# Where the matmul operands of a decoder layer start in SBUF: gaps between pools

## The chip, the cores and the metric

One NeuronCore of a Trainium2 chip runs the whole kernel as one program. The metric is device time in microseconds, the median of several runs. Before the change it is 1307.95 us (3 runs, 1306.92 to 1308.1). The profiled execution took 1307.29 us by the clock of the runs; the span from its first to its last instruction is 1305.5 us, so 1.8 us lie around the span.

## The reference, cut to what matters

One decoder layer in float32 on 1024 tokens plus 16 meta tokens (L = 1040), width 1024:

```
a    = rmsnorm(h, ln_mix_pre);  proj = a @ w_in            # 1024 x 3584
mix  = concat(diff_attention(...), hgrn2(...)) @ w_out      # 1024 x 1024: the output projection
h    = h + rmsnorm(mix, ln_mix_post)
a    = rmsnorm(h, ln_ffn_pre)
u    = causal_depthwise_conv3(a @ w_up) + conv_b            # 1024 x 5632: the up stage
gate, up = split(u)
y    = (gelu(gate) * up) @ w_down                           # 2816 x 1024: the down stage
out  = h + rmsnorm(y, ln_ffn_post), meta rows dropped
```

## The kernel before, in words

**Split products.** Every large matrix product runs in float32r, with both operands split into a high part and a low part. A product of a stationary operand S and a moving operand M is three matmuls into one PSUM bank: S high with M high, S high with M low, S low with M high (or with the roles exchanged). They always stand next to each other in the program, and each matmul loads its own 128 columns of stationary operand (512 bytes in each partition) ahead of itself: 'PEld' in the profile is that load, 'PE' the matmul.

**The stages on TensorE**, in the order of the program:

- The input projection (L234, L236, L238): the weights are stationary, the normalized activations `ahi` and `alo` move, 272 or 384 columns at a time. A row of `ahi` is 1040 floats, 4160 bytes, so that from one of its 8 rows k to the next the start moves by 64 bytes modulo 512. Attention and HGRN heads are interleaved with it.
- The output projection (`out_part`, L1012, L1014, L1016): blocks of the mixed heads (`mp`, loaded back from DRAM into X1, X2 or the pool `mixload`; `m7` in the pool `early`) are stationary, `w_out` moves, 512 columns at a time. Its first half (`out_first`) is interleaved with the last HGRN head; the second half alternates with a residual and norm chain (`post`, `trans`).
- The up stage (`unit`, L1378 to L1380): one level of Strassen's scheme (Winograd's form). For each of 21 tiles `ft` and both column groups p there are seven products j = 0 to 6 of 12 matmuls. Weights `uh`, `ul` (pools `weights` and `sums`, in turns) are stationary; the activation tile `t{p}_{j}` moves. A tile holds 4 rows of high parts and then 4 rows of low parts. For p = 0 a row has 258 columns, for p = 1 it has 256. The tiles lie in several pools: `early` (e0, e1), the `mix` tiles X0, X1, X2, `tsplit` and `tsplit2`. The p = 1 tile in X0, `t1_6`, is stored with rows of 258 columns, of which 256 are used.
- `plain_unit` (L1359 to L1361) computes tile ft = 0 without the scheme while the sums for the seven tiles are still being made.
- The down stage (L1536 to L1538): again seven products, 77 steps of 12 matmuls; the gated activations `gh`, `gl` (pool `down`) are stationary, the weights `wh`, `wl` (pool `weights`) move, 512 columns at a time. 924 matmuls in all.

**What sets the addresses.** A tile pool takes SBUF when it is opened, from the left end or the right end, next to the pool that was opened before on that side and is still open. Inside a pool the tiles stand one behind the other in the order in which they are first asked for. So one tile's size decides where everything behind it starts. Nearly every tile is a multiple of 512 bytes in each partition or a known remainder above it, so the distance between two operands modulo 512 is fixed for a whole stage.

**The word distance below** is the start of the moving operand minus the start of the stationary operand, in bytes within a partition, modulo 512. It is worked out from the addresses in the built program, which the profile does not show. As one row of weights is 512 bytes and one weight tile 2048, it is the same for the stationary operand that is used and the one that is loaded next, as long as the tile stays the same.

Of the kernel before, what the change touches and what calls it, by code (L numbers as in the profile page):

```python
# [9 lines left out]
F32 = mybir.dt.float32  # L10
F32R = mybir.dt.float32r
# [6 lines left out]
P = 128  # L18
META = 16
SEQ = 1024  # L20
L = META + SEQ
D = 1024
KD = D // P
# [8 lines left out]
WN = [258, 256]  # L32
# [53 lines left out]
def layer_kernel(ctx: ExitStack, tc: tile.TileContext, x, meta, table, lbl, gpre, gpost, win,  # L86
# [25 lines left out]
    def const(shape, name, dt=F32):  # L112
        return cp.tile(shape, dt, tag=name, name=name)
# [12 lines left out]
    nlam = const([P, 1], "nlam")  # L126
    cwt = const([P, 2 * NF, 3], "cwt")
    cbt = const([P, 2 * NF], "cbt")
    m0 = const([P, 152], "m0", F32R)[:, :46]
    G.memset(m0.bitcast(F32), 0.0)  # L130
    m0_7 = const([P, 2, 1, 2], "m0_7", F32R)

# [33 lines left out]

    mx_cm, mxp = pool("mix", 1)

    def long_tile(name):
        return mxp.tile([P, 8, WN[0]], F32, tag="X0", name=name).rearrange("p a c -> p (a c)")  # L170

    def parts_tile(name):
        return mxp.tile([P, 2, 384], F32R, tag="ms", name=f"ms{name}", bufs=2)
# [7 lines left out]
    ws_cm, wsp = pool("wdsums", 6)  # L181
    at_cm, atp = pool("at", 1)
    ahi = atp.tile([P, KD, L], F32R, tag="ahi", name="ahi")
    alo = atp.tile([P, KD, L], F32R, tag="alo", name="alo")

    last_load, lows = [], []

# [59 lines left out]
    xts, xss = {}, {}  # L247

    def spare_tile(tag):
        return mxp.tile([P, 8, WN[0]], F32, tag=tag, name=f"{tag}_in").rearrange("p a c -> p (a c)")  # L250
# [527 lines left out]
    t_a, tiles = attn_in(0)  # L778
    grow = zp.tile([P, D], F32, tag="xt", name="grow", bufs=3)[:1]
    SY.dma_start(grow, gpre)  # L780
    spare = [spare_tile(t) for t in ("X1", "X2", "X0")]
    load_x(0)
    load_x(1)
    load_x(2, spare[2][:, :D])
# [219 lines left out]
    def tok(i):  # L1004
        return (2, 14) if i == 0 else (P, start(i))
# [27 lines left out]
    def block_tile(n, i):  # L1033
        tag = SLOTS[n][i - 1]
        if tag == "mp":
            return mlp.tile([P, 2, KD, P], F32R, tag="mp", name=f"mp{n}_{i}")
        t = mxp.tile([P, 8, WN[0]], F32R, tag=tag, name=f"mp{n}_{i}")
        return t.rearrange("p a c -> p (a c)")[:, : 2 * KD * P].rearrange("p (l k t) -> p l k t", l=2, k=KD)
# [64 lines left out]
    def ps_b(name):  # L1103
        return pp.tile([P, 512], F32, tag="b", name=name)
# [3 lines left out]
    e_cm, ep = pool("early", 1, "right")  # L1108
# [7 lines left out]
    q_cm, qp = pool("p2", 2, "right")  # L1116
# [63 lines left out]
    xhs = {}  # L1180

    def load_xh(i):
        r = tok(i)[0]
        if i:
            xhs[i] = qp.tile([P, D], F32, tag="xh", name=f"xh{i}")
        else:
            both = ep.tile([P, 2 * D], F32, tag="e0", name="xh0")
            xhs[i], xhs["sum"] = both[:, :D], both[:, D:]
# [50 lines left out]
    tt = [[None] * 8 for _ in range(2)]  # L1239

    def t_tiles(p, j, where, tag):
        if len(tag) == 1:
            both = where.tile([P, 8, WN[p]], F32R, tag=tag[0], name=f"t{p}_{j}")
            return both[:, 0:4], both[:, 4:8]
        both = where.tile([P, 8, int(tag[1])], F32R, tag=tag[0], name=f"t{p}_{j}")
        return both[:, 0:4, : WN[p]], both[:, 4:8, : WN[p]]

    def t_split(p, j, src, where, *tag):
        hi, lo = t_tiles(p, j, where, tag)
        A.copy(hi, src)  # L1250
        V.tensor_tensor(lo, src, hi.bitcast(F32), op=ALU.subtract)
        tt[p][j] = (hi, lo)

    def quarter(p, j):
        n = WN[p]
        a, c = {0: (0, 0), 7: (0, n), 4: (4, 0), 6: (4, n)}[j]
        return at2[p][:, a:a + 4, c:c + n]

    def t_sums(p, where, last):
        b11, b12, b21, b22 = (quarter(p, j) for j in (0, 7, 4, 6))  # L1260
        V.tensor_tensor(b11, b12, b11, op=ALU.subtract)
        V.tensor_tensor(b12, b22, b12, op=ALU.subtract)
        V.tensor_tensor(b22, b22, b11, op=ALU.subtract)
        t_split(p, 1, b22, where, f"t{p}_1")
        t_split(p, 2, b11, where, f"t{p}_2")
        t_split(p, 3, b12, where, f"t{p}_3")
# [10 lines left out]
    for i in range(1, NBLK):  # L1277
        py = ps_b(f"py1_{i}")
        if i >= 3:
            y0_gain(i)  # L1280
        if i == 1:
            load_xh(1)
            load_xh(0)
        if i + 1 < NBLK:
            second_load(i + 1)
            load_xh(i + 1)
        run(blocks[i], py, wo, range(4), True, False)
        if i == 3:
            trans(1)
        run(blocks[i], py, wo, range(4, 7 if i == 1 else 8), False, i > 1)  # L1290
        if i > 3:
            trans(i - 2)
        if i == 5:
            trans(0)
        if i == 1:
            pm = ps_b("py1_0")
            for _ in meta_part(pm, wo, True):
                pass
            for p in range(3):
                out_last(p)  # L1300
# [12 lines left out]
        if i == 5:  # L1313
            t_split(0, 0, quarter(0, 0), ep, "e0")
            t_split(0, 4, quarter(0, 4), ep, "e1")
        if i == 7:
            t_split(0, 7, quarter(0, 7), mxp, "X2", WN[0])
            t_split(0, 6, quarter(0, 6), mxp, "X1", WN[0])
        if i in (2, 3):
            for p in (1 + 2 * i, 2 + 2 * i):  # L1320
                out_last(p)
    close(q_cm, ml_cm, y_cm, wo_cm, ws_cm)

    xu_cm, xup = pool("xu", 2)
    t_cm, tp = pool("tsplit", 1)

    marks = {}

# [19 lines left out]
    def plain_unit(p, bank):  # L1348
        n = WN[p]
        us = outputs(0, p)  # L1350
        for col in range(2):
            for side in range(2):
                pt = bank(f"pq{p}_{col}{side}")[:, :n]
                for kh in range(2):
                    hi, lo = plain[f"{side + 1}{kh + 1}"]
                    th, tl = tt[p][(0, 4, 7, 6)[2 * col + kh]]
                    for k in range(4):
                        s = slice(P * k, P * (k + 1))
                        T.matmul(pt, hi[:, s], th[:, k], start=(kh + k == 0), stop=False)  # L1359
# [54 lines left out]
        next(p0)  # L1414
    trans(8)
    t_split(1, 7, quarter(1, 7), tp, "t1_5")
    t_split(1, 6, quarter(1, 6), mxp, "X0", WN[0])
    t_sums(0, tp, (mxp, "X2", WN[0]))
# [269 lines left out]
```

## Time and profile before

| | |
|---|---|
| median of 3 runs | 1307.95 us |
| profiled execution | 1307.29 us; span 1305.5 us |
| PE busy | 1277.2 us, 98% of the span, 10154 matmuls |
| PEld busy | 1182.0 us, 91% |
| DVE, ACT, POOL busy | 884.8, 696.5, 482.9 us |
| input projection with attention and HGRN | span 0 to 507 us |
| output projection, first and second half | 507 to 566 and 566 to 625 us |
| sums and plain units | 625 to 655 us |
| up stage | 655 to 1078 us |
| down stage and end | 1078 to 1305.5 us |

A row of the timeline has the start in us, the duration in us, the engine, the line, the operation, the names written and read (with the numbers of buffers left out) and the shape. The duration of a matmul contains its passage through the array, some 0.17 us, which overlaps with its neighbours; the rate at which TensorE works is read from start to start. Starts are printed to 0.01 us, so a rate is taken over a dozen matmuls or more. A row of a table by stretch has the length of the stretch, then for each engine its busy time and number of instructions, then the granted TensorE clock and the share and rate of the DMA engines.

### The profile page before, as it was taken

How to read it: one execution, taken by the hardware profiler on the slowest of the kernel's cores; microseconds unless marked ns; L12 is line 12 of the kernel's file. 1: busy time of each engine (PE TensorE's matmuls, PEld its weight loads, DVE VectorE, ACT ScalarE, POOL GpSimd, SP SyncE). 2: the span in 40 equal slices, each digit the busy share in tenths (PEclk: the TensorE clock that was granted, in tenths of full speed). 3: DMA queues.
4: the chain of work that ended last, by engine and by line, in shares of the span. 5: the costliest groups of instructions: out<-in, count | busy, mean ns of one | idle time of the engine just before them, and what ended most of it. 6: DMA issues, size and time to landing. Idle time of an engine off the chain costs nothing.

```text
span 1305.5 us, 26100 instructions
## 1 busy us (share of the span) xinstructions
PE 1277.2 (98%) x10154; PEld 1182.0 (91%) x10154; DVE 884.8 (68%) x1488; ACT 696.5 (53%) x1639; POOL 482.9 (37%) x387
## 2 busy tenths in 40 slices
PE   8999999999999999999999999999999999999997
PEld 7999999899999998767999999999999997888875
DVE  7574647465645574548997877877877767697586
ACT  8565466546644763447754444544544544454553
POOL 5231423242323310352076666566576631010121
PEclk9999999999999999999999999999999999999999
DMA  5243655183643533687222222222222137955263
GB/s 214 94 100 87 125 116 114 57 157 79 116 128 69 122 109 109 224 270 261 91 75 89 82 74 73 90 75 81 90 74 81 57 122 268 318 188 168 82 210 121
DMA packets 116418, 165.04 MB, mean 126 GB/s; under 512 B 10099, under 2 KB 57523, under 8 KB 116294
## 3 DMA queue, kind: packets, MB, share of 16 engines
q1 hardware_dynamic: 93062, 151.84, 35.6%
q0 software_dynamic: 23232, 11.54, 7.5%
q8 instruction: 80, 1.31, 0.4%
q14 instruction: 44, 0.36, 0.1%
HBM read 134.24 MB, written 52.17 MB: 143 GB/s over the span
## 4 chain that ended last, share of the span: by engine, by line
PE 81%; DVE 6%; DMA 4%; ACT 4%; issue 2%; SPq 0%; POOL 0%; DVEq 0%; ACTq 0%; POOLq 0%
PE pd L1537 5%; PE pd L1536 5%; PE pd L1538 5%; PE pb L1378 4%; PE pb L1380 4%; PE pb L1379 4%; PE pa L1378 3%; PE pa L1380 3%; PE pa L1379 3%; PE pc L1378 3%; PE pc L1379 3%; PE pc L1380 3%; PE pa L732 3%; PE pi_hf L234 1%; DMA ra<-in_wup_dram 1%
## 5 line engine op out<-in xcount | busy, mean ns | idle before, releaser
L1378 PE MATMUL pb<-t,uh 128*128 128x258 f32 x504 | 142.3, 282 | 2.5 <-DVE u L53 2.5
L1379 PE MATMUL pb<-t,uh 128*128 128x258 f32 x504 | 141.6, 281 | 0.0
L1380 PE MATMUL pb<-t,ul 128*128 128x258 f32 x504 | 141.6, 281 | 0.0
L1537 PE MATMUL pd<-wl,gh 128*128 128x512 f32 x308 | 122.0, 396 | 1.1 <-DVE wl L53 1.1
L1536 PE MATMUL pd<-wh,gh 128*128 128x512 f32 x308 | 121.8, 395 | 0.1
L1538 PE MATMUL pd<-wh,gl 128*128 128x512 f32 x308 | 121.7, 395 | 0.0
L53 DVE SCALAR_TENSOR_TENSOR c<-uu,cwt,c 128x514 f32<-128x514 f32 (+1 forms) x88 | 97.2, 1104 | 19.6 <-ACT c L53 18.9
L53 POOL TENSOR_TENSOR c<-c,c 128x514 f32<-128x514 f32 (+1 forms) x44 | 63.8, 1449 | 122.4 <-ACT c L53 120.4
L1378 PEld LDWEIGHTS pb<-t,uh 128*128 128x128 f32 x504 | 95.5, 189 | 3.0 <-DVE u L53 2.9
L1379 PEld LDWEIGHTS pb<-t,uh 128*128 128x128 f32 x504 | 95.5, 189 | 0.0
L1378 PE MATMUL pa<-t,uh 128*128 128x258 f32 (+1 forms) x336 | 95.2, 283 | 0.0
L1380 PEld LDWEIGHTS pb<-t,ul 128*128 128x128 f32 x504 | 95.2, 189 | 0.0
L1380 PE MATMUL pa<-t,ul 128*128 128x258 f32 (+1 forms) x336 | 95.1, 283 | 0.0
L1379 PE MATMUL pa<-t,uh 128*128 128x258 f32 (+1 forms) x336 | 94.8, 282 | 0.0
L1378 PE MATMUL pc<-t,uh 128*128 128x258 f32 (+1 forms) x336 | 94.4, 281 | 0.0
L1379 PE MATMUL pc<-t,uh 128*128 128x258 f32 (+1 forms) x336 | 94.0, 280 | 0.0
L1380 PE MATMUL pc<-t,ul 128*128 128x258 f32 (+1 forms) x336 | 93.7, 279 | 0.0
L53 DVE SCALAR_TENSOR_TENSOR c<-ug,cwt,c 128x514 f32<-128x514 f32 (+1 forms) x88 | 88.3, 1005 | 1.4 <-ACT c L53 0.6
L53 ACT CAST uh<-ra 128x512 fp32r<-128x512 f32 x67 | 41.1, 616 | 62.2 <-PE pb L1379 41.1
L53 POOL TENSOR_TENSOR ul<-ws,uh 128x512 fp32r<-128x512 f32 x42 | 60.5, 1440 | 35.5 <-ACT uh L53 34.8
L1537 PEld LDWEIGHTS pd<-wl,gh 128*128 128x128 f32 x308 | 57.7, 187 | 16.4 <-DVE wl L53 2.6
L53 DVE TENSOR_TENSOR ul<-ra,uh 128x512 fp32r<-128x512 f32 x42 | 38.7, 921 | 49.4 <-ACT uh L53 49.4
(388 smaller groups left out, 4166.3 us busy)
## 6 DMA issues: line engine op xcount, KB each, us to landing
ra<-in_wup_dram SPq DMA_DIRECT2D x88, 256.0 KB, 2.7
mp<-msc SPq DMA_DIRECT2D x23, 512.0 KB, 5.0
tsc<-in_wdown_dram SPq DMA_DIRECT2D x44, 256.0 KB, 4.8
wi<-tsc SPq DMA_DIRECT2D x44, 256.0 KB, 2.8
gi<-gsc SPq DMA_DIRECT2D x33, 256.0 KB, 5.3
wi<-in_wdown_dram SPq DMA_DIRECT2D x33, 256.0 KB, 5.3
gsc<-c SPq DMA_DIRECT2D x22, 257.0 KB, 2.1
tsc<-in_wdown_dram POOLq DMA_DIRECT2D x22, 256.0 KB, 7.5
```

The costliest lines, as they stand in the source:

```text
L53: ins = call(*args, **kw)
L234: T.matmul(pt, hi[:, s], ahi[:, k, t0:t1], start=(k == 0), stop=False)
L732: T.matmul(po[:, :P], w_, vn[:, j], start=(j == 0), stop=(j == i))
L1378: T.matmul(pt, hi[:, s], th[:, k], start=(first and k == 0), stop=False, skip_group_check=True)
L1379: T.matmul(pt, hi[:, s], tl[:, k], start=False, stop=False, skip_group_check=True)
L1380: T.matmul(pt, lo[:, s], th[:, k], start=False, stop=(k == 3), skip_group_check=True)
L1536: T.matmul(py, gh[:, s], wh, start=(k == 0 and pr not in (3, 7)), stop=False, skip_group_check=True)
L1537: T.matmul(py, gh[:, s], wl, start=False, stop=False, skip_group_check=True)
L1538: T.matmul(py, gl[:, s], wh, start=False, stop=(k == NH - 1), skip_group_check=True)
```

## The change

No instruction is added, removed or moved: on PE, DVE, ACT, POOL and SP the rows stand in the same order. Two rows, the split of `t1_6`, have 1024 columns in one piece in place of 4 x 256. Four tiles of ACT's queue and one load on SP carry other waits, because memory is handed over from other predecessors. The rest is addresses:

```diff
-    m0 = const([P, 152], "m0", F32R)[:, :46]
+    m0 = const([P, 72], "m0", F32R)[:, :46]
...
+    MIX = {"X0": 2064, "X1": 2176, "X2": 2064}
+
+    def mix_tile(tag, dt, name):
+        return mxp.tile([P, MIX[tag]], dt, tag=tag, name=name)
+
+    def gap(where, name, n):
+        where.tile([P, n // 4], F32, tag=name, name=name, bufs=1)
...
-    spare = [spare_tile(t) for t in ("X1", "X2", "X0")]
+    spare = {n: spare_tile(t) for n, t in ((2, "X0"), (0, "X1"), (1, "X2"))}
...
     wo_cm, wop = pool("wo", 7)
+    gap(wop, "gap0", 448)
+    ml_cm, mlp = pool("mixload", 1)
     y_cm, yp = pool("y0", 1)
-    ml_cm, mlp = pool("mixload", 1)
...
-    m7 = ep.tile([P, 8, 2, P], F32R, tag="e1", name="m7")
+    xh0 = ep.tile([P, 2 * D], F32, tag="e0", name="xh0")
+    m7 = ep.tile([P, 8 * WN[0]], F32R, tag="e1", name="m7")[:, 16:].rearrange("p (b l t) -> p b l t", b=8, l=2)
...
     def t_tiles(p, j, where, tag):
-        if len(tag) == 1:
-            both = where.tile([P, 8, WN[p]], F32R, tag=tag[0], name=f"t{p}_{j}")
-            return both[:, 0:4], both[:, 4:8]
-        both = where.tile([P, 8, int(tag[1])], F32R, tag=tag[0], name=f"t{p}_{j}")
-        return both[:, 0:4, : WN[p]], both[:, 4:8, : WN[p]]
+        tag, n = (tag + (8 * WN[p],))[:2]
+        both = where.tile([P, n], F32R, tag=tag, name=f"t{p}_{j}")[:, :8 * WN[p]].rearrange("p (a c) -> p a c", a=8)
+        return both[:, 0:4], both[:, 4:8]
...
     t_cm, tp = pool("tsplit", 1)
+    gap(tp, "gap1", 64)
...
     t2_cm, t2p = pool("tsplit2", 1)
+    gap(t2p, "gap2", 320)
...
     v_cm, cv = pool("conv", 2, "right")
+    gap(cv, "gap3", 224)
     dn_cm, dn = pool("down", 4, "right")
```

What that makes of the distances, from the addresses of the two built programs:

| matmuls | columns | distance before | distance after |
|---|---|---|---|
| up stage, `t1_0`, `t1_4`, `t1_5` | 256 | 256 | 448 |
| up stage, `t1_1`, `t1_2`, `t1_3` | 256 | 448 | 448 |
| up stage, `t1_6` | 256 | 384, growing by 8 a row | 448 |
| up stage, `t0_2`, `t0_5` (first row) | 258 | 320 | 0 |
| up stage, `t0_6` | 258 | 256 | 0 |
| up stage, `t0_3` | 258 | 384 | 64 |
| up stage, `t0_0`; `t0_1`; `t0_4` | 258 | 448; 256; 384 | 384; 448; 448 |
| down stage, all | 512 | 288 | 0 |
| output projection | 512 | 192 (135 matmuls), 352 (99), 128 (93), 64 (27), 256 (18), 416 (12) | 0 (264 matmuls), 64 (120) |
| input projection | 272, 384 | each of 0, 64, ... 448 for one of the 8 k | the same eight, two places further |

In a tile of 258 columns a row is 1032 bytes, so the distance grows by 8 from row to row, and the low parts lie 32 further than the high parts. The weights stay where they were; 28 matmuls of the output projection with `m0` and `m0_7` have distances of their own. The one place where the waits of a queue differ by more than that load is on ACT, at the splits that make the p = 0 tiles `t0_*` of the up stage from the transposed activations `at2_0` (between them stand copies of the plain units' banks `pq` into `ug` and `uu`). Before:

```order
L53 CAST t1_0_7680<-at2_1_6971 128x1024
L53 CAST t1_4_7683<-at2_1_6971 128x1024
L53 CAST t0_1_7785<-at2_0_6975 128x1032 [waits DVE_49,Pool_49]
L53 COPY ug0_0_7640<-pq0_10_7712 128x258 [waits PE_49]
L53 CAST t0_2_7788<-at2_0_6975 128x1032
L53 CAST t0_3_7791<-at2_0_6975 128x1032 [waits DMAHW6_49,DVE_49]
L53 CAST t0_5_7795<-at2_0_6975 128x1032 [waits PE_49]
L53 COPY uu0_0_7641<-pq0_11_7738 128x258 [waits PE_49]
```

And now, at the same place:

```order
L53 CAST t1_0_7682<-at2_1_6972 128x1024
L53 CAST t1_4_7685<-at2_1_6972 128x1024
L53 CAST t0_1_7787<-at2_0_6976 128x1032 [waits DMAHW6_49,DVE_49]
L53 COPY ug0_0_7642<-pq0_10_7714 128x258 [waits PE_49]
L53 CAST t0_2_7790<-at2_0_6976 128x1032 [waits Pool_49]
L53 CAST t0_3_7793<-at2_0_6976 128x1032
L53 CAST t0_5_7797<-at2_0_6976 128x1032 [waits DVE_49,PE_49]
L53 COPY uu0_0_7643<-pq0_11_7740 128x258 [waits PE_49]
```

The rows stand in the same order; the wait for a load queue has come from `t0_3` forward to `t0_1`, the wait for POOL goes from `t0_1` to `t0_2`, and the wait for DVE from `t0_3` to `t0_5`.

More of the change, by code (lines that the diff above doesn't have):

```diff
@@ L167, in layer_kernel @@
     mx_cm, mxp = pool("mix", 1)
+    MIX = {"X0": 2064, "X1": 2176, "X2": 2064}
[3 more added lines that the diff above has]
+        where.tile([P, n // 4], F32, tag=name, name=name, bufs=1)
     def long_tile(name):
-        return mxp.tile([P, 8, WN[0]], F32, tag="X0", name=name).rearrange("p a c -> p (a c)")
+        return mix_tile("X0", F32, name)
     def parts_tile(name):
@@ L179, in parts_store @@
                          m[:, l, off:off + P * n].bitcast(F32).rearrange("p (b c) -> p b c", c=P))
-    ws_cm, wsp = pool("wdsums", 6)
+    ws_cm, wsp = pool("wosplit", 6)
     at_cm, atp = pool("at", 1)
-    ahi = atp.tile([P, KD, L], F32R, tag="ahi", name="ahi")
-    alo = atp.tile([P, KD, L], F32R, tag="alo", name="alo")
+    ahi, alo = (atp.tile([P, KD, L], F32R, tag=t, name=t) for t in ("ahi", "alo"))
     last_load, lows = [], []
@@ L249, in spare_tile @@
     def spare_tile(tag):
-        return mxp.tile([P, 8, WN[0]], F32, tag=tag, name=f"{tag}_in").rearrange("p a c -> p (a c)")
+        return mix_tile(tag, F32, f"{tag}_in")
     def load_x(i, where=None):
@@ L1036, in block_tile @@
             return mlp.tile([P, 2, KD, P], F32R, tag="mp", name=f"mp{n}_{i}")
-        t = mxp.tile([P, 8, WN[0]], F32R, tag=tag, name=f"mp{n}_{i}")
-        return t.rearrange("p a c -> p (a c)")[:, : 2 * KD * P].rearrange("p (l k t) -> p l k t", l=2, k=KD)
+        return mix_tile(tag, F32R, f"mp{n}_{i}")[:, : 2 * KD * P].rearrange("p (l k t) -> p l k t", l=2, k=KD)
     def block_load(m, i, k0, k1):
@@ L1186, in load_xh @@
         else:
-            both = ep.tile([P, 2 * D], F32, tag="e0", name="xh0")
-            xhs[i], xhs["sum"] = both[:, :D], both[:, D:]
+            xhs[i], xhs["sum"] = xh0[:, :D], xh0[:, D:]
         SY.dma_start(xhs[i][:r], meta[14:16, :] if i == 0 else x[P * (i - 1): P * i, :])
@@ L1263, in t_sums @@
         V.tensor_tensor(b22, b22, b11, op=ALU.subtract)
-        t_split(p, 1, b22, where, f"t{p}_1")
-        t_split(p, 2, b11, where, f"t{p}_2")
-        t_split(p, 3, b12, where, f"t{p}_3")
+        for j, b in ((1, b22), (2, b11), (3, b12)):
+            t_split(p, j, b, where, f"t{p}_{j}")
         V.tensor_tensor(b21, b21, b22, op=ALU.subtract)
@@ L1316, in layer_kernel @@
         if i == 7:
-            t_split(0, 7, quarter(0, 7), mxp, "X2", WN[0])
-            t_split(0, 6, quarter(0, 6), mxp, "X1", WN[0])
+            t_split(0, 7, quarter(0, 7), mxp, "X2", MIX["X2"])
+            t_split(0, 6, quarter(0, 6), mxp, "X1", MIX["X1"])
         if i in (2, 3):
@@ L1321, in layer_kernel @@
                 out_last(p)
-    close(q_cm, ml_cm, y_cm, wo_cm, ws_cm)
+    close(q_cm, y_cm, ml_cm, wo_cm, ws_cm)
     xu_cm, xup = pool("xu", 2)
     t_cm, tp = pool("tsplit", 1)
+    gap(tp, "gap1", 64)
     marks = {}
@@ L1416, in layer_kernel @@
     t_split(1, 7, quarter(1, 7), tp, "t1_5")
-    t_split(1, 6, quarter(1, 6), mxp, "X0", WN[0])
-    t_sums(0, tp, (mxp, "X2", WN[0]))
+    t_split(1, 6, quarter(1, 6), mxp, "X0", MIX["X0"])
+    t_sums(0, tp, (mxp, "X2", MIX["X2"]))
     close(a_cms.pop())
     t2_cm, t2p = pool("tsplit2", 1)
+    gap(t2p, "gap2", 320)
     p1 = plain_unit(1, ps_b)
```

## The prediction

> **What bounds the kernel now.** I read the page first, then the table by stretch, then TensorE's timeline inside the two stages that hold most of the time. Only addresses change, so the question is where the rate of the matmuls sets the end, and whether that rate knows addresses at all. The page's busy line, its clock line, the costliest group of the up stage and one of the three of the down stage:
>
> ```profile
> PE 1277.2 (98%) x10154; PEld 1182.0 (91%) x10154; DVE 884.8 (68%) x1488; ACT 696.5 (53%) x1639; POOL 482.9 (37%) x387
> PEclk9999999999999999999999999999999999999999
> L1378 PE MATMUL pb<-t,uh 128*128 128x258 f32 x504 | 142.3, 282 | 2.5 <-DVE u L53 2.5
> L1537 PE MATMUL pd<-wl,gh 128*128 128x512 f32 x308 | 122.0, 396 | 1.1 <-DVE wl L53 1.1
> ```
>
> TensorE is busy 98% of the span at full clock, and in front of these two groups it stood idle for 2.5 and 1.1 us in all. So in the up and the down stage the end is set by how fast one matmul follows the other. The stretches of the output projection's two halves, of the up stage and of the down stage:
>
> ```profile
> 507.00:566.00 59.00, 58.35 (x698) 45.62 (x697) 28.04 (x56) 23.12 (x63) 12.95 (x13) 1.00 0.68 215
> 566.00:625.00 59.00, 56.15 (x264) 43.04 (x264) 41.89 (x44) 37.16 (x109) 26.11 (x18) 1.00 0.81 267
> 655.00:1078.00 423.00, 420.50 (x3539) 419.98 (x3538) 322.58 (x467) 205.88 (x365) 264.35 (x182) 1.00 0.25 83
> 1078.00:1300.00 222.00, 216.87 (x924) 172.37 (x923) 165.69 (x241) 109.53 (x219) 26.79 (x17) 1.00 0.58 193
> ```
>
> In the up stage PE is busy for 420.5 of 423 us, DVE, the next, for 322.6, or 76%. A gain of 3% on PE leaves DVE at 79%: no other engine takes over. In the down stage DVE has 166 of 222 us. In the second half of the output projection PE is busy for 56.15 of 59 us only, with the DMA engines at 0.81; there a faster matmul partly meets a later wait.
>
> **Does the rate know the address?** The timeline of one round of the up stage (ft = 3), where each product begins; 12 matmuls lie between two rows:
>
> ```profile
> 697.61 0.28 PE L1378 MATMUL pc<-t,uh 128*128 128x256 f32 x1
> ...
> 699.03 0.28 PE L1378 MATMUL pa<-t,uh 128*128 128x258 f32 x1
> ...
> 700.47 0.28 PE L1378 MATMUL pa<-t,uh 128*128 128x256 f32 x1
> ...
> 701.91 0.28 PE L1378 MATMUL pb<-t,uh 128*128 128x258 f32 x1
> ...
> 703.35 0.28 PE L1378 MATMUL pb<-t,uh 128*128 128x256 f32 x1
> ...
> 704.76 0.28 PE L1378 MATMUL pc<-t,uh 128*128 128x258 f32 x1
> ...
> 706.18 0.28 PE L1378 MATMUL pc<-t,uh 128*128 128x256 f32 x1
> ...
> 707.54 0.29 PE L1378 MATMUL pb<-t,uh 128*128 128x258 f32 x1
> ...
> 708.99 0.28 PE L1378 MATMUL pb<-t,uh 128*128 128x256 f32 x1
> ...
> 710.37 0.29 PE L1378 MATMUL pa<-t,uh 128*128 128x258 f32 x1
> ```
>
> In order: `t1_6` takes 1.42 us (118.3 ns a matmul), `t0_0` 1.44 (120), `t1_0` 1.44 (120), `t0_1` 1.44 (120), `t1_1` 1.41 (117.5), `t0_2` 1.42 (118.3), `t1_2` 1.36 (113.3), `t0_3` 1.45 (120.8), `t1_3` 1.38 (115). Shape and number of matmuls are the same for all tiles of 256 columns, and yet they take 113.3 to 120 ns. The bank doesn't explain it (`t1_1` and `t1_3` share pb at 117.5 and 115; `t1_6` and `t1_2` share pc at 118.3 and 113.3). The distance explains most: the three tiles at 448 are the three fastest. It doesn't explain all: at the same 448 one tile takes 117.5 and one 113.3, so there are at least two states, and which one a product falls into depends on how it is entered.
>
> At 512 columns, one stretch of the down stage (distance 288; 24 matmuls) and three of the output projection:
>
> ```profile
> 1150.01 0.40 PE L1537 MATMUL pd<-wl,gh 128*128 128x512 f32 x1
> 1150.01 0.19 PEld L1538 LDWEIGHTS pd<-wh,gl 128*128 128x128 f32 x1
> ...
> 1155.61 0.39 PE L1537 MATMUL pd<-wl,gh 128*128 128x512 f32 x1
> ```
>
> ```profile
> 577.28 0.39 PE L1016 MATMUL pz<-woh,m 128*128 128x512 f32 x1
> ...
> 580.02 0.40 PE L1016 MATMUL pz<-woh,m 128*128 128x512 f32 x1
> ...
> 585.62 0.39 PE L1016 MATMUL py<-woh,mp 128*128 128x512 f32 x1
> ...
> 610.29 0.39 PE L1012 MATMUL py<-woh,mp 128*128 128x512 f32 x1
> ...
> 614.94 0.39 PE L1016 MATMUL py<-woh,mp 128*128 128x512 f32 x1
> ```
>
> The second row is the load of the next matmul's weights: it begins with the running matmul. The down stage goes at 5.60 / 24 = 233.3 ns. The first two rows of the projection span 12 matmuls at distance 64: 2.74 / 12 = 228.3, and as starts are rounded to 0.01 us, 228.3 +- 0.8. The next pair spans 24 at distance 192: 5.60 / 24 = 233.3. The last pair spans 20 at distance 128: 4.65 / 20 = 232.5. So with 512 columns the rate falls as the distance goes from 192 over 128 to 64. The lowest rate that any product holds, 113.3 ns for 256 columns, doubled is 226.7 for 512: I take that as the floor.
>
> One row speaks against carrying this on to distance 0. The input projection visits each distance for three matmuls (384 columns) and is at 0, then at 64:
>
> ```profile
> 127.62 0.33 PE L234 MATMUL pi_hg<-ahi,wh_hg 128*128 128x384 f32 x1
> ...
> 128.15 0.33 PE L234 MATMUL pi_hg<-ahi,wh_hg 128*128 128x384 f32 x1
> ...
> 128.66 0.34 PE L234 MATMUL pi_hg<-ahi,wh_hg 128*128 128x384 f32 x1
> ```
>
> At 0 three take 0.53 us, 177 ns each, 7 above the floor of 170 (113.3 x 1.5); at 64 they take 0.51, at the floor. Three matmuls after a change of distance are no steady state, but 0 isn't better than 64 here.
>
> **The change part by part.**
>
> *Down stage, 924 matmuls, 288 to 0.* No row shows 512 columns at 0. Bounds: 226.7 (the floor) and 233.3 + 3.4 = 236.7 (7 over the floor as in the input projection, rounded up by its 3 ns of reading error). I take the nearest distance with the same width in a steady run: 64, and of its 228.3 +- 0.8 the upper part, 229, because of the row against. Gain 924 x 4.3 = 4.0 us; bounds +6.1 and -3.1.
>
> *Up stage, tiles of 256 columns.* One nanosecond on one of the seven products is 12 x 21 = 252 ns. The three tiles at 448 average (117.5 + 113.3 + 115) / 3 = 115.3, and I let all seven have that. Today `t1_0` has 120 and `t1_6` 118.3; `t1_4` and `t1_5`, at the distance of `t1_0`, I put between, at 119.3. Gain (120 + 118.3 + 2 x 119.3 - 4 x 115.3) x 0.252 = 3.9 us. Bounds: all at 117.5 gives (476.9 + 345.8 - 822.5) x 0.252 = 0.05; all at 113.3 gives 7.4 us.
>
> *Up stage, tiles of 258 columns.* `t0_0`, `t0_1` and `t0_4` exchange distances that are there today (120, 120, 120.8): nothing. `t0_2`, `t0_5`, `t0_6` go to 0 and `t0_3` to 64, which no tile of 258 has. They have 118.3, 118.3 (same distance), 120 (that of `t0_1`) and 120.8 now, 477.4 together. Bounds: 114.2 each (the floor by width) is +5.2 us; 120.8 each, the worst row, is -1.5 us. I take the middle, 117.5: +1.9 us.
>
> *Output projection.* 384 matmuls from about 232.5 (two thirds at 192 and 352, the rest mixed) to 229: 1.3 us. The second half waits for other things too, and the first is chopped up by HGRN's small matmuls; I count half, 0.7 us. Bounds 0 and 2.
>
> *Input projection, attention, HGRN.* The same eight distances in another order: nothing, +-0.5 us. *Sums and plain units* (625 to 655 us): hidden behind DVE, which makes the sums. *The waits on ACT* (`t0_1` for the load queue a few rows sooner): the load is one of earlier blocks, hidden; if not, it delays the first unit by some part of a microsecond, in a stretch where DVE is late anyway. The other form of `t1_6`'s split has the same number of elements: nothing.
>
> *What is late next.* The 2.5 us for DVE at the start of the up stage and the 1.1 us at the start of the down stage grow where PE arrives sooner: 0.3 us lost.
>
> Sum: 4.0 + 3.9 + 1.9 + 0.7 - 0.3 = 10.2 us. The profiled execution took 1307.29 (span 1305.5), which gives 1297.1; the median of the runs is 0.7 above it, so **1297.7 us**.
>
> **What the Trainium skill says against it.** "TensorE: Matmul & The Clock Gate", in "Step-by-step: what each phase is for", gives TensorE two independent read ports, so that loading weights takes nothing from the running matmul; "SBUF — State Buffer", in "Who interferes with whom", says that PE never waits on anyone. By these the address is without effect, and the change does nothing. By the formula in "Back-to-back issue gap" of the first page a matmul of 512 columns takes 215.7 ns and one of 256 takes 109, whatever the address. The trace disagrees: 233.3 and 113.3 to 120, and the latter differ at one shape.
>
> **The rivals.**
>
> *The address does nothing.* Then the spread in the round above belongs to the place in the round, and all stays: 1308 us. For it: two tiles at one distance differ by 4.2 ns. Against it: the steady 228.3, 232.5 and 233.3 of the projection, at one shape and in one loop.
>
> *The states fall the slow way.* All seven tiles settle at the 117.5 of `t1_1` (gain 0), the tiles of 258 stay as they are, and the down stage gets part of what the input projection's row leaves, say 231: 924 x 2.3 = 2.1 us, and 0.5 from the projection. That is 1305.3 us. For it: the state depends on the way in, and every way in changes. Against: two of three tiles at 448 found the fast state, from different ways in.
>
> *Equal addresses collide: slower.* Place: the down stage, where the load of the next weights begins with the matmul (1150.01 above) and both now start at the same byte modulo 512. Price by the input projection's upper reading: 236.7, -3.1 us, with the 258 tiles that go to 0 at 120.8, -1.5, the other tiles at 117.5, 0, nothing from the projection: 1312.6 us. It decides once the down stage passes 233.3 by more than the rest gains, 6.2 / 924 = 6.7 ns, or by anything if the rest gains nothing. For it: 177 against 170 ns at 0. Against: the fall from 192 to 64.
>
> **How the numbers follow.** The forecast 0.63, the slow states 0.20, no effect 0.07, collision 0.10. A measurement of this kernel can tell about 0.2%, 2.6 us, from no change; faster by that means below 1305.3. The forecast's cases are all there; the slow states come out at that very border, so half of them: 0.73. The other half and no effect: 0.17; collision: 0.10. All gains at their best together would be 20 us; that needs four lucky answers, so the lower end is the forecast less 7, 1290.5. The upper end takes in most of the slow states: 1306.5.
>
> **What would show it.** Right: down stage rows 229 ns apart, the same in all 77 steps; `t1_0` and `t1_4` to `t1_6` at 113 to 118; rows of the input projection as before. Wrong: rows 233 or more apart in the down stage (step one), or all seven tiles at 117.5 or more (step two), or tiles of 258 above 120. If the rows are faster and the end isn't, then PE's waits for DVE in the up stage have grown by more than 0.3 us.

## The result, and the profile after

The changed kernel takes **1301.40 us** (median of 6 runs, 1300.19 to 1302.68), the kernel before, run beside it, 1307.11 (6 runs, 1306.4 to 1308.1): a ratio of 0.9956, 95% interval 0.9944 to 0.9969, so 5.7 us less, or 0.44%. Forecast were 1297.7 us and 10.2 us less. The profiled execution has a span of 1298.9 us against 1305.5. By stage, from the first matmul of each to its last, in the two profiled executions:

| stage | before | after | difference | forecast |
|---|---|---|---|---|
| input projection, attention, HGRN | 475.6 | 476.0 | +0.4 | 0 |
| output projection | 122.2 | 122.4 | +0.2 | -0.7 |
| sums and plain units | 25.3 | 24.9 | -0.5 | 0 |
| up stage | 421.75 | 420.30 | -1.45 | -5.8 + 0.3 for waits |
| down stage | 217.90 | 212.49 | -5.4 | -4.0 |

The changed kernel's page (engine, busy us, share, instructions; then two of its costliest groups). The code has moved, so that L1383 to L1385 are the former L1378 to L1380 and L1543 to L1545 the former L1536 to L1538:

```profile
PE 1268.1 (98%) x10154; PEld 1179.0 (91%) x10154; DVE 887.0 (68%) x1488; ACT 695.1 (54%) x1639; POOL 482.6 (37%) x387
...
L1383 PE MATMUL pb<-t,uh 128*128 128x258 f32 x504 | 142.5, 283 | 2.9 <-DVE u L53 2.7
L1544 PE MATMUL pd<-wl,gh 128*128 128x512 f32 x308 | 120.5, 391 | 2.0 <-DVE wl L53 2.0
```

Its table by stretch (up stage, down stage, the projection's second half):

```profile
655.00:1078.00 423.00, 420.06 (x3546) 417.46 (x3545) 326.15 (x470) 206.03 (x367) 264.10 (x182) 1.00 0.24 83
1078.00:1300.00 222.00, 209.38 (x919) 171.75 (x917) 165.78 (x241) 108.33 (x217) 26.71 (x17) 0.99 0.58 197
566.00:625.00 59.00, 55.07 (x263) 42.91 (x263) 41.30 (x44) 37.29 (x107) 26.85 (x18) 1.00 0.81 268
```

The down stage's matmuls went from a mean of 396 to 391 ns; the stage gave more than forecast. The up stage gave a quarter of its forecast, and neither of its rows says why: the wait for DVE ahead of L1383 is 2.7 us against 2.5, PE's busy time 420.06 against 420.50. The starts of its products do. The changed kernel's round ft = 3, one row for the first matmul of each product, as the prediction showed it of before:

```profile
699.16 0.29 PE L1383 MATMUL pa<-t,uh 128*128 128x258 f32 x1
...
700.62 0.28 PE L1383 MATMUL pa<-t,uh 128*128 128x256 f32 x1
...
701.99 0.28 PE L1383 MATMUL pb<-t,uh 128*128 128x258 f32 x1
...
703.42 0.28 PE L1383 MATMUL pb<-t,uh 128*128 128x256 f32 x1
...
704.84 0.28 PE L1383 MATMUL pc<-t,uh 128*128 128x258 f32 x1
...
706.26 0.28 PE L1383 MATMUL pc<-t,uh 128*128 128x256 f32 x1
...
707.62 0.28 PE L1383 MATMUL pb<-t,uh 128*128 128x258 f32 x1
...
709.05 0.28 PE L1383 MATMUL pb<-t,uh 128*128 128x256 f32 x1
```

`t1_0` now takes 1.37 us (114 ns a matmul; before 120), `t1_1` 1.42 (118), `t1_2` 1.36 (113). This round is faster, as forecast. But only every second one is. The changed kernel in round 6, at the seam between `t1_2` and `t0_3`, first on TensorE (the matmuls and one load of weights), then on DVE:

```profile
766.95 0.28 PE L1385 MATMUL pc<-t,ul 128*128 128x256 f32 x1
767.23 0.19 PEld L1383 LDWEIGHTS pb<-t,uh 128*128 128x128 f32 x1 [0.20 <-DVE u L53]
767.23 0.39 PE L1383 MATMUL pb<-t,uh 128*128 128x258 f32 x1
767.45 0.29 PE L1384 MATMUL pb<-t,uh 128*128 128x258 f32 x1
```

```profile
757.32 0.42 DVE L53 TENSOR_TENSOR uu<-pb,x 128x256 f32<-128x256 f32 x1
...
763.77 2.46 DVE L53 SCALAR_TENSOR_TENSOR c<-ug,cwt,c 128x510 f32<-128x510 f32 x2
766.16 0.68 DVE L53 TENSOR_TENSOR ul<-ws,uh 128x512 fp32r<-128x512 f32 x1
766.76 0.75 DVE L53 TENSOR_TENSOR u<-pb,x 128x258 f32<-128x258 f32 x2
```

The matmul at 767.23 starts 0.28 us after the one ahead of it, not 0.11, and the next follows after 0.22 in place of 0.12. Product 3 writes on into bank pb, and DVE must first have read product 1's sum from there: `u2`, the first of the two at 766.76. That sum alone takes 0.41 us by the trace, so it ends at about 767.17. What waits for it is the load of the first matmul's weights: it would have run beside the matmul at 766.95, and begins at 767.23, 0.05 us after the sum's end. From 757.32 to the end of the `u` pair no row of DVE shows idle time: two taps of the convolution, the weight split `ul` (0.68 us, for the next round) and then `u2` stand behind each other. The same place in the kernel before, on TensorE and on DVE:

```profile
767.23 0.28 PE L1380 MATMUL pc<-t,ul 128*128 128x256 f32 x1
767.23 0.19 PEld L1378 LDWEIGHTS pb<-t,uh 128*128 128x128 f32 x1
767.34 0.29 PE L1378 MATMUL pb<-t,uh 128*128 128x258 f32 x1
767.46 0.28 PE L1379 MATMUL pb<-t,uh 128*128 128x258 f32 x1
```

```profile
766.13 0.68 DVE L53 TENSOR_TENSOR ul<-ws,uh 128x512 fp32r<-128x512 f32 x1
766.73 0.74 DVE L53 TENSOR_TENSOR u<-pb,x 128x258 f32<-128x258 f32 x2
```

There `u2` ended at about 767.14. The matmul came at 767.34, 0.2 us later, but the load of its weights runs one matmul ahead and began at 767.23, 0.08 us after the sum. As such a load followed the sum's end by 0.05 us where it waited, the room was 0.03 us here and nothing in rounds 8, 12, 14 and 20, and the tables of before call nothing there a wait. PE gained more than that. The changed kernel's table of PE's waits in the up stage gives this place as before (us in total, times, longest):

```profile
PE pb L1383 <- DVE u L53: 2.7, 2, 1.4
```

Two times, 2.7 us, both at the start of the stage. The pauses in ten later rounds, about 0.3 us from start to start, aren't in it, because a matmul is drawn 0.28 us long, its passage included, and so covers most or all of the pause. The same table for the loads does show them; before, then the changed kernel:

```profile
PEld pb L1378 <- DVE u L53: 2.9, 2, 1.6
PEld pb L1383 <- DVE u L53: 5.3, 12, 1.6
```

**Theory** for the experiments: the down stage brings nearly the whole result; in the up stage the addresses are worth what the prediction said for the tiles of 256 columns, and 3 us of it are lost at `u2`. **Rivals**: both stages bring about half; or DVE as a whole has no room, so that the order of its queue doesn't matter.

### The profile page after: what moved, and what is told of

Read it like the earlier page. It is cut to its first block, busy times and chain, and to the rows that moved or that the text cites. A ratio compares the mean times of both kernels' runs of the same rounds, so it can differ in the third digit from the quotient of the medians.

```text
span 1298.9 us, 26100 instructions
## 1 busy us (share of the span) xinstructions
PE 1268.1 (98%) x10154; PEld 1179.0 (91%) x10154; DVE 887.0 (68%) x1488; ACT 695.1 (54%) x1639; POOL 482.6 (37%) x387
## 4 chain that ended last, share of the span: by engine, by line
PE 46%; DVE 4%; ACT 2%; issue 1%; DMA 1%; DVEq 0%; ACTq 0%
PE pd L1544 5%; PE pd L1545 5%; PE pd L1543 5%; PE pb L1383 5%; PE pb L1384 4%; PE pb L1385 4%; PE pa L1384 3%; PE pa L1383 3%; PE pa L1385 3%; PE pc L1384 3%; PE pc L1383 3%; PE pc L1385 3%; DVE c L53 1%; DVE t L53 1%; DVE xh L53 1%
## 5 line engine op out<-in xcount | busy, mean ns | idle before, releaser
L1383 PE MATMUL pb<-t,uh 128*128 128x258 f32 x504 | 142.5, 283 | 2.9 <-DVE u L53 2.7
L1385 PE MATMUL pb<-t,ul 128*128 128x258 f32 x504 | 141.0, 280 | 0.0
L1545 PE MATMUL pd<-wh,gl 128*128 128x512 f32 x308 | 120.0, 390 | 0.0
L1543 PE MATMUL pd<-wh,gh 128*128 128x512 f32 x308 | 120.0, 390 | 0.0
L53 POOL TENSOR_TENSOR c<-c,c 128x514 f32<-128x514 f32 (+1 forms) x44 | 63.8, 1449 | 122.3 <-ACT c L53 120.2
L1383 PEld LDWEIGHTS pb<-t,uh 128*128 128x128 f32 x504 | 95.0, 189 | 5.3 <-DVE u L53 5.3
L1385 PEld LDWEIGHTS pb<-t,ul 128*128 128x128 f32 x504 | 95.3, 189 | 0.0
L1383 PE MATMUL pa<-t,uh 128*128 128x258 f32 (+1 forms) x336 | 94.6, 281 | 0.0
L1385 PE MATMUL pa<-t,ul 128*128 128x258 f32 (+1 forms) x336 | 94.3, 281 | 0.0
L1385 PE MATMUL pc<-t,ul 128*128 128x258 f32 (+1 forms) x336 | 94.1, 280 | 0.0
L1383 PE MATMUL pc<-t,uh 128*128 128x258 f32 (+1 forms) x336 | 93.9, 279 | 0.0
```

The lines of the kernel that those rows point to most:

```text
L53: ins = call(*args, **kw)
L1383: T.matmul(pt, hi[:, s], th[:, k], start=(first and k == 0), stop=False, skip_group_check=True)
L1385: T.matmul(pt, lo[:, s], th[:, k], start=False, stop=(k == 3), skip_group_check=True)
L1543: T.matmul(py, gh[:, s], wh, start=(k == 0 and pr not in (3, 7)), stop=False, skip_group_check=True)
L1545: T.matmul(py, gl[:, s], wh, start=False, stop=(k == NH - 1), skip_group_check=True)
```

## The experiments

### 1 and 2: the two halves of the change

Distance 0 in the down stage alone, on the kernel before; and the changed kernel without it:

```diff
     v_cm, cv = pool("conv", 2, "right")
+    gap(cv, "gap3", 224)
```

> The kernel before with one gap more, so that the down stage has distance 0 in place of 288; nothing else is moved. Theory (the down stage alone brings nearly all of the result; 924 matmuls at 226.7 in place of 233.3 ns, less a longer wait for the weight split on DVE): 5.4 us less than before, so 1301.7, with the up stage at 421.8 us as before. Rival (the down stage brings only half of it, the rest comes from the other parts): 3 us less, 1304.

> The changed kernel without the gap ahead of the down stage, which therefore stays at distance 288. Theory (the faster matmuls of the up stage meet a new wait for DVE, and the output projection ends at the same time as before): 0.3 to 1.5 us less than before, 1305.6 to 1306.8. Rival (up stage and projection bring what the prediction gave them): 5 us less, 1302.

Measured: the first 1303.41 us against 1307.37 (ratio 0.9971, interval 0.9962 to 0.9980: 3.8 us less, 2.6 to 5.0); the second 1305.77 (0.9988, 0.9979 to 0.9997: 1.6 us less, 0.4 to 2.7). The sum, 5.4, is close to the 5.7 of the whole change. By the totals alone the first lies between theory and rival. By the stages it doesn't: with the gap alone the down stage is 212.5 us and the up stage 421.7, without it 217.65 and 420.4: each stage takes what it takes in the kernel (before or changed) whose addresses it has. What blurs the totals is the stage ahead: its matmuls are the same in all kernels of a kind, and in the 14 profiled executions of this study it took 475.6 to 479.6 us. A change of a few us is read in its own stage.

### 3 and 4: `u2` first, by the order of the code

In the changed kernel and, as a control, in the kernel before, the call that prepares the next weights is put behind the units' step:

```diff
         for j in range(7):
-            prep(7 * (ft + 1) + j)
+            if j != 1:
+                prep(7 * (ft + 1) + j)
             for u in units:
                 next(u)
+            if j == 1:
+                prep(7 * (ft + 1) + j)
```

> The changed kernel; in each round of the up stage DVE now makes u2 (product 3's second PSUM sum, for which TensorE waits in the changed kernel) ahead of the weight split ul of the next round, instead of behind it. Addresses and work are the same. Theory (the gain of the up stage is eaten by that one place in DVE's queue): the pause of about 0.28 us ahead of the first matmul of product 3 goes away in all rounds, up stage 3 us shorter, 417 us; whole kernel 3 us less than the changed kernel, 1298.4. Rival (DVE has no room: the wait only moves to the next product or to the weights): up stage within 0.7 us of 420.3, 1301.4.

> The same exchange on DVE's queue in the kernel before, with its addresses. Theory (at the old addresses TensorE comes to that place about 0.2 us later than DVE is done, so nothing waits there): the same time as before within 0.5 us, 1307.1. Rival (the old order costs something whatever the addresses): 2 to 3 us less than before, 1304.5.

Measured: 1302.05 us (0.9965, 0.9952 to 0.9978) and 1309.26 us (1.002, 1.001 to 1.003). The pauses were all still there, up stage 420.7 us. That looks like the rival, but it is no test: the program's scheduler places DVE's instructions itself, and from the second round on it had put `ul` ahead of `u2` again. Only the first round was reordered, and there it cost: 23.40 us against 23.01 with the new addresses, 24.81 against 22.97 with the old ones. These 1.8 us are the 1.9 us by which the control is slower than before. Most of them are not the wait itself. In the first round TensorE waits a second time, ahead of product 5, 2.65 us from start to start with the new order, at the new and at the old addresses (1.7 with the old order). In experiment 4 the granted clock then falls to 0.50 for 3.41 us, and more than a dozen matmuls follow each other at 0.21 us in place of 0.12; in experiment 3 it stays at 1.00. The same 3 us of the table by stretch, experiment 3, then 4:

```profile
677.00:680.00 3.00, 3.00 (x27) 3.00 (x26) 2.05 (x4) 1.33 (x2) 2.32 (x3) 1.00 0.24 90
677.00:680.00 3.00, 3.00 (x16) 3.00 (x15) 2.05 (x3) 0.95 (x2) 2.27 (x2) 0.50 0.23 87
```

### 5 and 6: `ul` bound behind `u2`

On top of the edit of experiments 3 and 4:

```diff
             if j == 1:
-                prep(7 * (ft + 1) + j)
+                with tc.issue_after(marks[ft, 1].ins):
+                    prep(7 * (ft + 1) + j)
```

> The changed kernel; the weight split ul of the next round's product 1 is now bound to stand behind both u2 on DVE's queue, in all rounds (the run before this one moved it in the first round only). Addresses and work are the same. Theory (0.7 us of ul ahead of u2 is what TensorE, now faster, waits for in every second round): the pauses of 0.27 to 0.32 us ahead of the first matmul of product 3 are gone, up stage 420.3 less ten times 0.28, so 417.5 us; whole kernel 2.8 us less than the changed kernel, 1298.6. Rival (the pause moves to another place of the same round, because DVE's convolution taps are what is late): up stage within 0.7 us of 420.3, 1301.4.

> The same binding of ul behind u2 in the kernel before, at the old addresses. Theory (at the old rate TensorE reaches product 3 about 0.2 us after DVE is done, so there is nothing to gain): up stage 421.7 us within 0.5, whole kernel 1307.4 within 1. Rival (the order of DVE's queue is worth the same at any address): up stage 419 us, 1304.6.

Measured: with the new addresses 1299.58 us (0.9938, 0.9923 to 0.9953), with the old ones 1309.29 (1.0012, 1.0000 to 1.0024). The second misses its expected 1307.4 within 1. The totals mix two things, a slower first round (24.86 and 24.60 us; both profiled executions have the 3.41 us at a clock of 0.50) and the rounds behind it. The rounds from 3 to 21 are read from the start of round 3 to that of round 21, 18 rounds. The last of these rows for before (the first, 699.03, stands in the prediction), the last for the changed kernel (the first, 699.16, above), then both for the kernel with the old addresses and the binding, and both for the new addresses with it:

```profile
1057.88 0.28 PE L1378 MATMUL pa<-t,uh 128*128 128x258 f32 x1
```

```profile
1056.79 0.29 PE L1383 MATMUL pa<-t,uh 128*128 128x258 f32 x1
```

```profile
700.92 0.28 PE L1378 MATMUL pa<-t,uh 128*128 128x258 f32 x1
...
1059.72 0.28 PE L1378 MATMUL pa<-t,uh 128*128 128x258 f32 x1
```

```profile
701.97 0.29 PE L1383 MATMUL pa<-t,uh 128*128 128x258 f32 x1
...
1056.81 0.29 PE L1383 MATMUL pa<-t,uh 128*128 128x258 f32 x1
```

Before: (1057.88 - 699.03) / 18 = 19.94 us a round. The changed kernel: 19.87, in fact 19.71 and 19.99 to 20.06 in turns. Old addresses with the binding: 19.93, no gain, as the theory said (its 0.2 us of room is 0.03 by the load). New addresses with the binding: 19.71 in every round, with a start of 0.11 us at each seam. So the addresses are worth 0.22 us a round, 4.5 us in 20 rounds; in the changed kernel 20 x 0.155 = 3.1 us of that goes to the place in DVE's queue. Both rivals fall: the pause doesn't move elsewhere, and the same order is worth nothing at the old addresses. The expected 417.5 us of up stage was missed (419.0), by the first round's 1.85 us.

### 7: what sets the two rates at distance 448

After the change `t1_1` and `t1_4` stay at 118.0 ns, the other tiles of 256 columns at 113.3 to 114.7. Both stand behind a tile of 258 columns at distance 448. So that tile is moved away for one of the two, on top of experiment 5:

```diff
+    gap(tp, "gap4", 64)
     t_sums(0, tp, (mxp, "X2", MIX["X2"]))
...
-    gap(t2p, "gap2", 320)
+    gap(t2p, "gap2", 256)
```

> As the kernel with ul behind u2 and the new addresses, with 64 bytes more ahead of t0_1, t0_2, t0_3 (distances 0, 64, 128 in place of 448, 0, 64) and 64 fewer behind them; the tiles of 256 columns stay at 448. Theory (which of the two rates a product at 448 takes is set by the distance of the tile ahead of it; behind a tile at 448 it stays at 118 ns): t1_1 goes from 118.0 to 113.3, while t1_4, still behind a tile at 448, stays at 118.0; 12 x 21 x 4.7 ns = 1.2 us of the up stage, 416.3 us if the kernel with ul behind u2 has 417.5. t0_1 itself 118.2 as t0_2 has at distance 0 now, 0.3 us more. Rival (the rate belongs to the place in the round or to the PSUM bank): t1_1 stays at 118.0, up stage as without the 64 bytes.

Measured: 1300.79 us (0.9944, 0.9931 to 0.9957), and an up stage of 419.7 us against 419.0 in experiment 5. `t1_1` (the two middle rows) went to 114.3 ns and `t1_4` stayed at 118.0: how a product is entered decides its rate. A tile at 448 ahead is not the only way into the slow one: in the kernel before, `t1_1` had 118 behind a tile at 256. But the round became longer, not shorter, (1056.39 - 700.83) / 18 = 19.75 us:

```profile
700.83 0.29 PE L1383 MATMUL pa<-t,uh 128*128 128x258 f32 x1
...
705.13 0.28 PE L1383 MATMUL pb<-t,uh 128*128 128x256 f32 x1
...
706.50 0.28 PE L1383 MATMUL pc<-t,uh 128*128 128x258 f32 x1
...
1056.39 0.29 PE L1383 MATMUL pa<-t,uh 128*128 128x258 f32 x1
```

`t0_1` at distance 0 takes 122.3 ns, not the expected 118.2; `t0_2` at 64 119.5 (118.2 at 0 before), `t0_3` at 128 120.9 (119.5 at 64), and `t1_3` behind it 114.7 (113.3). The tiles at 0 have two rates as well: 118.2 behind a product at 118.0 (`t0_2`, `t0_5`), 122.3 behind one at 113 to 115 (`t0_6`, and now `t0_1`). What `t1_1` gains, the three tiles of 258 columns that moved give back, and more. Here the rate of one tile could not be moved by itself.

### 8, 10, 11, 12: the distance in the down stage

Other gaps ahead of the down stage's pool give distances 64 (288 in place of 224), 448 (160) and 256 (480); in the other one the low activations alone are moved:

```diff
-    gap(cv, "gap3", 224)
...
+        if nm == "1_0":
+            gap(dn, "gap5", 224)
         gl = dn.tile([P, 512], F32R, tag="gl", name=f"gl{nm}")
```

> The changed kernel with distance 64 in the down stage. Theory (the rate follows the distance, and 0 is the best of all for 512 columns): 229 ns a matmul as in the projection at 64, down stage 2.1 us longer than the 212.5 us of distance 0. Rival (anything below 128 gives the floor in a long steady run): 226.7 ns, 212.5 us.

> The changed kernel; in the down stage the low activations gl start 288 bytes away, so that one matmul of three (wh against gl) is at distance 288 and the two others (wh and wl against gh) stay at 0. Theory A (what meets the moving operand is the load of the next weights that runs beside the matmul): the second matmul of each three (wl against gh, with the load of gl beside it) is the slow one, 233 ns or more from its start to the next, and the third is at 227. Theory B (a matmul's own stationary operand matters): the third is the slow one. Either way about 308 x 6.6 ns = 2.0 us more in the down stage, 214.5. Theory C (all matmuls between two kinds share the loss, as the rate is a state of the stream): all three alike at about 229.

> The changed kernel with distance 448 in the down stage, that of the tiles of 256 columns. Theory (the rate is lowest from 448 to 0 and rises on both sides): 226.7 to 228 ns, down stage 212.5 to 213.5 us. Rival (512 columns have their best at 0 and rise with the distance on either side, as with 64): 229 ns, 214.5 us.

> The changed kernel with distance 256 in the down stage. Theory (from 192 to 352 the rate is flat, and 256 lies between): 233.3 ns, down stage 218 us as before. Rival (half of 512 bytes is a second good distance, since the load's and the moving operand's rows then alternate): 229 or less, 214.5 us.

Each of the four was executed once, for its trace, so only stages and rates are read, not totals. Each pair of rows is 24 matmuls apart in the stage's steady part. The changed kernel, then the four in the order above:

```profile
1132.58 0.39 PE L1543 MATMUL pd<-wh,gh 128*128 128x512 f32 x1
...
1138.02 0.39 PE L1543 MATMUL pd<-wh,gh 128*128 128x512 f32 x1
```

```profile
1133.63 0.39 PE L1543 MATMUL pd<-wh,gh 128*128 128x512 f32 x1
...
1139.12 0.39 PE L1543 MATMUL pd<-wh,gh 128*128 128x512 f32 x1
```

```profile
1134.44 0.39 PE L1544 MATMUL pd<-wh,gh 128*128 128x512 f32 x1
...
1139.99 0.39 PE L1544 MATMUL pd<-wh,gh 128*128 128x512 f32 x1
```

```profile
1134.47 0.39 PE L1543 MATMUL pd<-wh,gh 128*128 128x512 f32 x1
...
1140.07 0.39 PE L1543 MATMUL pd<-wh,gh 128*128 128x512 f32 x1
```

```profile
1134.47 0.39 PE L1543 MATMUL pd<-wh,gh 128*128 128x512 f32 x1
...
1139.91 0.39 PE L1543 MATMUL pd<-wh,gh 128*128 128x512 f32 x1
```

| distance | 24 matmuls | each | down stage |
|---|---|---|---|
| 0 (changed kernel) | 5.44 us | 226.7 ns | 212.5 us |
| 64 | 5.49 | 229 | 214.1 |
| 0, 0 and 288 in turns | 5.55 | 231 | 216.3 |
| 448 | 5.60 | 233.3 | 217.4 |
| 256 | 5.44 | 226.7 | 212.5 |
| 288 (before) | 5.60 | 233.3 | 217.9 |

At 64 the theory held. At 448 theory and rival both fell: the best distance for 256 columns is as bad as 288 here. At 256 the rival held, and more than it asked: as good as 0; the reason that it gives (rows that alternate) isn't shown by that. The five distances agree with one that counts modulo 256: 0 and 256 give one rate, and 448 that of 192 in the projection before, 233.3. It is no slope either: 288, only 32 bytes past 256, has the full loss, 64 a third of it (and there the three kinds of matmul differ: 230.1, 227.0 and 229.8 ns in the order of the code).

In the kernel with `gl` moved, the mean time from a matmul's start to the next (the middle nine tenths of the 308 or 307 intervals of each kind) is 229.0 for `wh` against `gh`, 230.2 for `wl` against `gh`, and 234.9 for `wh` against `gl`, the one at 288. So theory A in its simple form falls: the matmul beside which `gl` is loaded isn't the slow one. The slow one has its own stationary operand at 288, as theory B says, but its two neighbours at distance 0 lose 2 to 4 ns as well, which is part of C (not all of it, as the three aren't alike). The stage took 216.3 us, 3.8 more than at 0, where 2.0 were expected.

### 9: the version that beats both

The binding of experiment 5 from the second round on, as an edit of that kernel:

```diff
-            if j != 1:
+            if ft == 1 or j != 1:
                 prep(7 * (ft + 1) + j)
...
-            if j == 1:
+            if ft > 1 and j == 1:
```

> The changed kernel with ul bound behind both u2 from the second round of the up stage on; the first round keeps its order. Theory (the binding is worth 3.1 us in rounds 2 to 21, and the 1.85 us that it cost were all in the first round, where the queues are still filling): first round 23.0 us as in the changed kernel, each later round 19.71, up stage 420.3 less 3.1, 417.2 us; whole kernel 1301.4 less 3.1, 1298.3, 9 us less than before. Rival (the first round's longer start comes back a round later): up stage 419.0 as with the binding in all rounds, 1299.6.

Measured: **1298.12 us** against 1307.95, ratio 0.9930, interval 0.9917 to 0.9944: about 9 us less (7 to 11). The first round takes 23.01 us, with the clock at 1.00, and the up stage 417.17: the theory held. Two rows of this kernel's PE, 18 rounds apart, then the seam of round 6 on PE and on DVE:

```profile
697.86 0.29 PE L1383 MATMUL pa<-t,uh 128*128 128x258 f32 x1
...
1052.70 0.29 PE L1383 MATMUL pa<-t,uh 128*128 128x258 f32 x1
```

```profile
765.34 0.28 PE L1385 MATMUL pc<-t,ul 128*128 128x256 f32 x1
765.45 0.28 PE L1383 MATMUL pb<-t,uh 128*128 128x258 f32 x1
```

```profile
761.93 2.45 DVE L53 SCALAR_TENSOR_TENSOR c<-ug,cwt,c 128x510 f32<-128x510 f32 x2
764.30 0.74 DVE L53 TENSOR_TENSOR u<-pb,x 128x258 f32<-128x258 f32 x2
764.97 0.67 DVE L53 TENSOR_TENSOR ul<-ws,uh 128x512 fp32r<-128x512 f32 x1
```

(1052.70 - 697.86) / 18 = 19.71 us. `u2` now ends at about 764.72, 0.6 us ahead of the load of the weights (beside the matmul at 765.34), and `ul` stands behind it.

## Why the prediction was right in its direction, and where its sizes were off

- *The rate knows the address.* Right. By the Trainium skill's page "TensorE: Matmul & The Clock Gate", section "Step-by-step: what each phase is for", the two read ports would keep it from that; here five sizes of one gap (none among them), with the same instructions, gave 226.7 to 233.3 ns.
- *Down stage, 924 matmuls at 229 ns, 4.0 us.* Mechanism right, size too small: 226.7 ns, 6.1 us of matmul time, of which the longer wait for `wl` (2.0 us in place of 1.1) takes 0.9; the stage is 5.4 us shorter. The value was taken from distance 64, and shaded up for the input projection's row at 0; 64 does have 229, but 0 has the floor. The three matmuls that follow a change of distance, on which the caution rested, weren't a steady state, as the prediction itself said of them.
- *Tiles of 256 columns at 115.3, 3.9 us.* Right in size: the seven together went from 823.0 to 804.9 ns, 18.1 x 0.252 = 4.6 us of matmul time. The two rates at 448 are still there; three tiles took the fast one, two the slow one, and two start slowly and reach it.
- *Tiles of 258 columns at 117.5, 1.9 us.* Wrong. Those that went to 0 and 64 have 118.2, 118.2, 122.3 and 119.5, together 478.2 against 477.4. The middle between two bounds, with no row near it, was no estimate; experiment 7 suggests that their rate hangs on the tile ahead of them too.
- *Waits grow by 0.3 us.* This is the step that failed: it was mis-sized more than tenfold: 3.1 us at `u2` and 0.9 at `wl`. I dismissed DVE by its 76% share of the stage and counted only the waits that the table of before showed. DVE has a stretch of 10 us without a gap in such a round (757.32 to 767.51 in the rows above), and `u2` is last in it, with 0.03 us of room for the load that waits for it. The prediction's last sentence, that faster rows without an earlier end would mean longer waits for DVE, was the right place to look, though the waits stand at the loads and not at the matmuls.
- *Output projection, 0.7 us.* Not seen. PE's busy time in the second half fell from 56.15 to 55.07 us and the stage took 122.4 us against 122.2. Over all profiled executions it took 121.0 to 122.2 at the old addresses (4, mean 121.56) and 120.4 to 122.4 at the new ones (10, mean 121.25), a difference no larger than their spread. It wasn't tried by itself.
- *Input projection: nothing.* It held: 477.4 us in the mean of the 4 and of the 10.
- *The rivals.* No effect is out. So is collision in the down stage: for 512 columns equal addresses are as good as any tried. But the sign "tiles of 258 above 120" came true: `t0_6`, at 0, went from 120.1 to 122.3 ns. "The states fall the slow way" was right for two of seven tiles.

Once one instruction on DVE stands behind two others, about 9 us are saved, near the 10.2 of the forecast. That nearness is partly luck: there is more of it in the down stage than forecast, and none in the tiles of 258 columns.

What stays open: the law behind the rates (of the distances seen, why 256 columns do better at 448 than at 256, and 512 columns best at 0 and 256). That the distance counts, and not where the moved operand itself starts, is argued and not tested: in the down stage the gap moves only the stationary operands, in the up stage only the moving ones move. Why the pause comes in every second round only is open too; it is DVE that alternates, at the old addresses as well, where in rounds 3 to 19 the load begins 0.50 to 0.53 us after `u2` in odd rounds and 0.05 to 0.08 in even ones. And the clock: it fell in the profiled executions of experiments 4 to 7, all with a wait of about 2.65 us in the first round, but not in that of experiment 3 with the same wait.

## What to carry to other kernels

When the limiting engine gets faster, look at each place where it waits on another and ask how much room was left there, not what share of the stage the other engine is busy; room that is not yet used up shows in no table of waits, only by laying the end of the one beside the start of the other, and for TensorE here that is the start of the weight load, one matmul ahead. Pauses shorter than a matmul's drawn length hide in PE's busy time, so read start to start, and ask for the waits of the loads. For long runs of 512-column float32r matmuls it pays to try a few paddings of one pool: 2.5% of the down stage here, for a gap that costs no instruction.

## What the hardware showed that I had not expected

- Matmuls of 512 columns take 226.7 ns at distances 0 and 256, 229 at 64, 233.3 at 288 and 448. Those of 256 columns take 119 to 120 at 256 and 113.3 to 118 at 448. The order of the distances is not the same for the two widths.
- At one distance a product of 12 matmuls goes at 113.3 or 118.0 ns, from its first matmuls or after at most four of them, and how it was entered sets which. A pause can change it: behind the seam in round 6 `t1_3` ran at 117.8 ns, as in four other rounds with the pause; in the other five, and in all rounds without it from the third on, at 113.2 to 114.8.
- A late load costs its whole delay, in two pieces: in round 6 the load came 0.27 us late, and the matmuls lost 0.16 us at the seam and another 0.10 until the second matmul; the slower `t1_3` behind it makes it 0.32 us in all.
- A wait of about 2.65 us was followed, in four of five profiled executions, by a fall of the granted clock to 0.50, for 3.41 us each time. The first round was 1.85 us longer with that (experiment 5) and 0.39 us longer without it (experiment 3), both at the new addresses.
